# The last output projection: all tiles of y kept on chip for both column halves, and the last tile in two halves

## The chip, the cores and the metric

One core of a Trainium2 chip runs the whole kernel. The metric is the device time of one execution in microseconds (us), as a median of runs. Beside it stands one profiled execution, from which all durations are read.

## What is computed

A two-layer backbone over 1024 latent tokens and 256 context tokens, 1024 wide. Layer 0 runs neighbourhood attention beside mLSTM heads, layer 1 runs 16 heads of a gated linear recurrence (HGRN2). Each layer ends in an output projection, a gate and the residual:

```python
def merge(o, z):                                   # layer 1
    o = _rms(jnp.swapaxes(o, 1, 2).astype(z.dtype), h_norm.reshape(HG_HEADS, HG_VDIM))
    return (o.reshape(o.shape[:2] + (HG_VW,)) * jax.nn.silu(z)) @ w_out     # (1024 x 2048) @ (2048 x 1024)
...
x = x + gate * y_lat
```

The change touches the last of these: `y @ w_out`, times the gate, plus x, for the 1024 latent tokens.

## The kernel before

The heads leave their result y transposed in DRAM (`yd2`: 16 heads, 128 rows of a head, 1024 tokens). The projection sums over 16 heads x 128 rows. It is cut in three ways: tokens in 8 tiles of 128 (`tt`), output columns in two halves of 512 (`b`, 1 before 0), the sum in two halves of 8 heads (`q`). The sums over the first 8 heads (q = 0) are made by `out_some` while the heads still run: for b = 1 they stay on chip in `acc`, for b = 0 they go to DRAM in `self.part`. The **last loop** (L1452 and on) does q = 1: first the 8 tiles of b = 1 with the weights `w2`, then the 8 tiles of b = 0 with `w1`.

float32 products are made exactly enough from two parts: `split` (L72) writes a value's rounded part with ScalarE (L74, `copy`) and the rest with VectorE (L75, subtraction), and each product is three matmuls (high x high, high x low, low x high; L745 to L747). A tile is therefore 8 heads x 3 = 24 matmuls of 128 x 128 by 512 columns into one PSUM bank.

`out_y` (L726) loads a tile of y in two pieces of 256 KB through SP's queue into raw buffers (`wraw`, 3 of them in the pool `yp`), and splits each into halves of `yh` and `yl` (2 buffers each). The weights of w1 arrive in the same three raw buffers of `yp`, two pieces (`later`) after each tile of b = 1. So y is loaded and split once for b = 1 and again for b = 0. `out_tile` (L761) then loads x (`oxh`, 3 buffers), and does three VectorE steps on 512 columns: PSUM plus `part` (L770), times the gate `gbc` (L772), plus x (L773). GpSimd's queue stores the tile (L1461).

Pools lie on two sides of the on-chip memory. `wp` and `yp` (with acc, w2, y's tiles, the raw buffers) are on the right. On the left the heads' pool `hg` is closed before the last loop, and the pools `op1` (`op`: oxh, og, gbc) and `wo1` (w1) open in its space. The heads' pool serves last as the raw buffers of w2.

The program is written in the order of the work. A scheduler places each engine's instructions by that order and by when it thinks that their operands are ready. It puts in all waits. Each engine, and each of the queues on which SP and POOL issue transfers, then runs in that fixed order.

Of the kernel before, what the change touches and what calls it, by code (L numbers as in the profile page):

```python
# [13 lines left out]
ALU = mybir.AluOpType  # L14
# [4 lines left out]
P = 128  # L19
D = 1024  # L20
KD = D // P
LAT = 1024
# [24 lines left out]
class Prog:  # L47
# [688 lines left out]
        return yh, yl  # L736


    def out_sum(self, ps, w, tt, qs, ysrc, yp, bufs, ys=None, rp=None):
        mm = self.nc.tensor.matmul  # L740
        for q in qs:
            yh, yl = ys[q] if ys else self.out_y(tt, q, ysrc, yp, bufs, rp)
            for k in range(8):
                kk = (q - qs[0]) * 8 + k
                mm(ps, lhsT=yh[:, k, :], rhs=w.h(kk), start=(kk == 0), stop=False)  # L745
                mm(ps, lhsT=yh[:, k, :], rhs=w.l(kk), start=False, stop=False)  # L746
                mm(ps, lhsT=yl[:, k, :], rhs=w.h(kk), start=False, stop=(kk == 8 * len(qs) - 1))  # L747

    def out_some(self, w, q, order, ysrc, yp, acc, dst):
        for tt in order:
            ps = self.ps("mm", [P, 512])
            self.out_sum(ps, w, tt, (q,), ysrc, yp, 2)
            o = self.t(yp, [P, 512], F32, "ox", 2) if acc is None else acc[:, tt, :]
            self.nc.scalar.copy(o, ps)
            if acc is None:
                self.nc.gpsimd.dma_start(out=dst[tt * P : (tt + 1) * P, 0:512], in_=o)


    def out_tile(self, w, b, tt, ysrc, xsrc, xt, yp, op, bufs, ys=None, part=None):  # L761
        nc = self.nc
        ps = self.ps("mm", [P, 512])
        self.out_sum(ps, w, tt, (0, 1) if part is None else (1,), ysrc, yp, bufs, ys)
        s = slice(b * 512, (b + 1) * 512)
        nc.sync.dma_start(out=xt, in_=xsrc[:, s])  # L766
        g = self.t(op, [P, 512], F32, "og", self.ogb)
        v = 1 if tt >= LAT // P else 0
        if part is not None:
            nc.vector.tensor_tensor(out=part, in0=ps, in1=part, op=ALU.add)  # L770
            ps = part
        nc.vector.tensor_tensor(out=g, in0=ps, in1=self.gbc[:, v, :], op=ALU.mult)  # L772
        nc.vector.tensor_tensor(out=xt, in0=xt, in1=g, op=ALU.add)  # L773


    def gate_bc(self, l, pool, nv, b):
# [433 lines left out]
    def build(self):  # L1210
        self.six = None
        tc, nc, a = self.tc, self.nc, self.a
        dma = nc.sync.dma_start
        with ExitStack() as es:
# [109 lines left out]
            with tc.tile_pool(name="ml", bufs=2) as pool, self.pp.phase(s=2, acc=2):  # L1324
                wq, self.six = {}, [(self.wp, "w", 4)] * 4
                with self.filler(), tc.issue_after(self.at[8]):
                    self.ml_ahead(*ML_AHEAD[-1])
                self.mask = self.t(pool, [P, 2, P], F32, "mmask", 1)
                dma(out=self.mask, in_=a["mmask"])

                def wo(q, b, ring=None):
                    if not ring:
                        ring, self.six = self.six[:8], self.six[8:] + self.six[:8]
                    src = a["woab"][q * D : (q + 1) * D, b * 512 : b * 512 + 512]
                    return self.wblock(None, "wo", [src], 8, 512, ring=ring)

                for g, at in self.ml_all(pool):
                    with self.filler(), tc.issue_after(at.ins):
                        if g in ML_AHEAD:
                            self.ml_ahead(*ML_AHEAD[g])  # L1340
                        if g == 7:
                            rh.close()
                            wr, self.ogb = es.enter_context(ExitStack()), 1
                            yp = wr.enter_context(tc.tile_pool(name="oy", bufs=1, side="right"))
                            acc = self.t(yp, [P, NT, 512], F32, "oacc", 1)
                            self.six = self.six + [(yp, "wo", 7)] * 7
                        for b in (1, 0):
                            if g == ML_OUT[b][0]:
                                wq[b] = wo(0, b)
                            for tt in [t for t, at_g in zip(ML_ORDER, ML_OUT[b]) if at_g == g]:  # L1350
                                self.out_some(wq[b], 0, [tt], self.yd, yp, acc if b else None, self.x1)
                w2 = wo(1, 1)
                self.gate_bc(0, yp, 2, 1)
                for tt in [8, 9, 3, 4, 2, 5, 1, 6, 0, 7]:
                    xt = self.t(yp, [P, 512], F32, "ox", 2)
                    self.out_tile(w2, 1, tt, self.yd, self.xin(tt), xt, yp, yp, 2, part=acc[:, tt, :])
                    nc.gpsimd.dma_start(out=self.x1[tt * P : (tt + 1) * P, 512:D], in_=xt)
            l0.close()
            l1 = es.enter_context(ExitStack())
# [1 line left out]
            with tc.tile_pool(name="op0", bufs=2) as op, ExitStack() as wl:  # L1361
                wl1 = wl.enter_context(tc.tile_pool(name="wo1", bufs=1))
                w1 = wo(1, 0, [(wl1, "wo", 8)] * 8)
                self.zero = self.t(lk, [P, CTX], F32, "gzero", 1)
                nc.vector.memset(self.zero, 0.0)
                self.lmask = self.t(lk, [P, 6, P], U8, "glm8", 1)
                self.lmask0 = self.t(lk, [P, P], F32, "glm0", 1)
                self.ident8 = self.t(lk, [P, P], U8, "ident8", 1)
                nc.vector.tensor_copy(self.ident8, self.ident)
                lm = self.t(op, [P, D], F32, "nx", 3)[:, 0 : 7 * P].rearrange("p (l f) -> p l f", f=P)  # L1370
                dma(out=lm, in_=a["glm"])
                nc.vector.tensor_copy(self.lmask, lm[:, 1:7, :])
                nc.vector.tensor_copy(self.lmask0, lm[:, 0, :])
                self.gate_bc(0, op, 2, 0)
                wr.close()
                right.close()
                self.six = None
                right = es.enter_context(ExitStack())
                self.wp = right.enter_context(tc.tile_pool(name="w1", bufs=2, side="right"))
                rh = right.enter_context(ExitStack())  # L1380
                self.open_h(rh)
                self.rawp = op
                self.slabs, self.ogb = 4, 3
                early = self.wblock(self.wp, "w", [a["wc"][0:512, 3 * 2048 : 3 * 2048 + 256]], 4, 256, op, ring=self.slabs)
                for tt in [8, 9, 4, 5, 6, 7, 0, 1, 2, 3]:
                    xt = self.t(op, [P, D], F32, "ox", 4)
                    dma(out=xt[:, 512:D], in_=self.x1[tt * P : (tt + 1) * P, 512:D])
                    part = self.t(op, [P, 512], F32, "og", 3)
                    dma(out=part, in_=self.x1[tt * P : (tt + 1) * P, 0:512])
                    self.out_tile(w1, 0, tt, self.yd, self.xin(tt), xt[:, 0:512], op, op, 2, part=part)  # L1390
                    if tt < 8:
                        nc.gpsimd.dma_start(out=self.x1[tt * P : (tt + 1) * P, 0:512], in_=xt[:, 0:512])
                    xn = self.t(op, [P, D], F32, "nx", 3)
                    self.norm(xn, xt, op)
                    self.mod_tr(1, [xn], tt, op, self.h_sink(tt * P, P))

            with l1:
# [48 lines left out]
                w2 = wo(1, 1, ring[4:], raw)  # L1446
            self.ogb = 4
            with tc.tile_pool(name="op1", bufs=2) as op, ExitStack() as wl:
                later = []
                wl1 = wl.enter_context(tc.tile_pool(name="wo1", bufs=1))  # L1450
                w1 = wo(1, 0, [(wl1, "wo", 8)] * 8, [yp, 3, "wraw"], later)
                for b, w in ((1, w2), (0, w1)):  # L1452
                    self.gate_bc(1, op, 1, b)
                    for tt in range(8):
                        xt = self.t(op, [P, 512], F32, "oxh", 3)
                        part = acc[:, tt, :]
                        if not b:
                            part = self.t(op, [P, 512], F32, "og", 4)
                            dma(out=part, in_=self.part[tt * P : (tt + 1) * P, :])
                        self.out_tile(w, b, tt, self.yd2, self.x1[tt * P : (tt + 1) * P], xt, yp, op, 2, part=part)  # L1460
                        nc.gpsimd.dma_start(out=a["out"][tt * P : (tt + 1) * P, b * 512 : (b + 1) * 512], in_=xt)  # L1461
                        for ld in later[:2]:
                            ld()
                        later = later[2:]
# [137 lines left out]
```

## Time and profile before

| | us |
|---|---|
| median of 3 runs | 3510.55 (3509.28 to 3517.46) |
| profiled execution, its own time | 3510.13 |
| its span, first to last instruction | 3508.3 |
| start of the last loop's first tile on TensorE | 3405.2 |
| last matmul starts | 3501.76 |

In the profile PE is TensorE's matmuls, PEld its weight loads, DVE VectorE, ACT ScalarE, POOL GpSimd and SP the engine that only issues transfers; SPq, POOLq and so on are their queues. A row of a timeline gives start, duration, engine, line, operation, written tile and read tiles, count, and in brackets how long the engine sat idle before it and what ended that. A row of windows gives the stretch, its length, the busy time of PE, PEld, DVE, ACT and POOL with counts of instructions, the clock that TensorE was granted (1.00 is full), the busy share of the DMA engines and what they moved in GB/s.

### The profile page before, as it was taken

The page shows a single profiled execution, that of the slowest core. Times are in us where ns is not written, and L with a number is a line of the kernel's source. Part 1 is how long each engine was busy: PE and PEld are TensorE (multiplying, and loading weights), DVE is VectorE, ACT ScalarE, POOL GpSimd, SP SyncE. Part 2 cuts the span into 40 slices and gives each one's busy share as a digit, 9 for nine tenths or more (in the row PEclk, how much of TensorE's full clock was granted, in tenths as well). Part 3 has the DMA queues.
Part 4 walks back from the last instruction along what each step waited for, and adds up shares of the span by engine and source line. Part 5 has one row for each costly group of instructions (what it writes and reads, how often), then busy time and mean ns, then how long its engine had stood idle before and what let it go on. Part 6 is the DMA issues. An engine that isn't in the chain of part 4 may idle for free. (4 is left out here: it accounts for less than half of the span.)

```text
span 3508.3 us, 64938 instructions
## 1 busy us (share of the span) xinstructions
PE 3453.9 (98%) x24438; PEld 3146.4 (90%) x24438; DVE 2374.5 (68%) x6009; ACT 1602.3 (46%) x3700; POOL 526.2 (15%) x844
## 2 busy tenths in 40 slices
PE   8999999999999999999999999999999999999999
PEld 5889999999999999988778999989999999999887
DVE  4668856766666654666767766577777767777855
ACT  5532135555445534555547333344444444444442
POOL 3211121222212211211211111000100000010010
PEclk9999999999999999999999999999999999999999
DMA  7552332332323235364484222211211221121346
GB/s 237 168 160 88 115 90 58 91 87 68 84 77 83 83 88 160 121 183 145 124 258 143 100 103 103 82 37 56 61 48 49 61 61 49 52 64 49 116 146 204
DMA packets 374409, 363.91 MB, mean 104 GB/s; under 512 B 30296, under 2 KB 323096, under 8 KB 373968
## 3 DMA queue, kind: packets, MB, share of 16 engines
q1 hardware_dynamic: 330096, 250.34, 24.4%
q0 software_dynamic: 44000, 109.42, 9.1%
q8 instruction: 193, 3.16, 0.4%
q14 instruction: 120, 0.98, 0.1%
HBM read 276.09 MB, written 83.42 MB: 102 GB/s over the span
## 5 line engine op out<-in xcount | busy, mean ns | idle before, releaser
L127 PE MATMUL mm<-wh,hh 128*128 128x256 f32 x2256 | 649.0, 288 | 4.6 <-DVE ev L922 2.7
L128 PE MATMUL mm<-wl,hh 128*128 128x256 f32 x2256 | 649.0, 288 | 1.9 <-DVE wl L75 1.8
L129 PE MATMUL mm<-wh,hl 128*128 128x256 f32 x2256 | 648.5, 288 | 0.0
L129 PE MATMUL mm<-hh,wl 128*128 128x512 f32 (+1 forms) x1344 | 491.5, 366 | 0.0
L127 PE MATMUL mm<-hh,wh 128*128 128x512 f32 (+1 forms) x1344 | 485.1, 361 | 0.0
L128 PE MATMUL mm<-hl,wh 128*128 128x512 f32 (+1 forms) x1344 | 483.6, 360 | 0.0
L127 PEld LDWEIGHTS mm<-wh,hh 128*128 128x128 f32 x2256 | 431.4, 191 | 12.7 <-issue 6.9
L128 PEld LDWEIGHTS mm<-wl,hh 128*128 128x128 f32 x2256 | 431.6, 191 | 7.2 <-DVE wl L75 2.7
L129 PEld LDWEIGHTS mm<-wh,hl 128*128 128x128 f32 x2256 | 431.1, 191 | 3.6 <-issue 0.7
L74 ACT CAST wh<-wraw 128x512 fp32r<-128x512 f32 x290 | 178.2, 620 | 263.1 <-PE mm L128 130.7
L128 PEld LDWEIGHTS mm<-hl,wh 128*128 128x128 f32 x1344 | 254.0, 189 | 32.0
L129 PEld LDWEIGHTS mm<-hh,wl 128*128 128x128 f32 x1344 | 253.9, 189 | 30.5 <-issue 0.2
L127 PEld LDWEIGHTS mm<-hh,wh 128*128 128x128 f32 x1344 | 254.3, 189 | 29.3
L1109 ACT COPY gksel<-gK 128x512 f32<-128x512 f32 x224 | 147.1, 663 | 218.9 <-PE s L1118 197.6
L75 DVE TENSOR_TENSOR wl<-wraw,wh 128x512 fp32r<-128x512 f32 x290 | 196.5, 686 | 51.9 <-ACT wh L74 49.4
L1118 PE MATMUL s<-gQ,gksel 128*128 128x128 f32 x1536 | 199.9, 276 | 0.0
L1118 PEld LDWEIGHTS s<-gQ,gksel 128*128 128x128 f32 x1536 | 192.4, 191 | 6.9
L745 PE MATMUL mm<-woh,yh 128*128 128x512 f32 x412 | 166.7, 405 | 6.7 <-ACT yh L74 6.5
L747 PE MATMUL mm<-woh,yl 128*128 128x512 f32 x412 | 165.3, 402 | 0.5 <-DVE yl L75 0.5
L746 PE MATMUL mm<-wol,yh 128*128 128x512 f32 x412 | 164.0, 399 | 0.0
L74 ACT CAST wh<-b 128x512 fp32r<-128x512 f32 x124 | 77.0, 622 | 187.1 <-PE sa L129 85.3
L1139 DVE TENSOR_TENSOR gQ<-gQ,gT 128x256 f32<-128x256 f32 x384 | 143.2, 414 | 26.1 <-PE s L1118 26.0
(456 smaller groups left out, 8491.9 us busy)
## 6 DMA issues: line engine op xcount, KB each, us to landing
wraw<-yd SPq DMA_DIRECT2D x144, 256.0 KB
wraw<-in_wc_dram SPq DMA_DIRECT2D x128, 256.0 KB
wraw<-in_wab_dram SPq DMA_DIRECT2D x98, 256.0 KB
md<-ev POOLq DMA_DIRECT2D x94, 256.0 KB, 2.8
adar<-in_wada_dram POOLq DMA_DIRECT2D x32, 512.0 KB, 4.9
b<-in_wc_dram SPq DMA_DIRECT2D x64, 256.0 KB
vzd<-qo POOLq DMA_DIRECT2D x56, 256.0 KB, 2.5
adar<-in_wada_dram SPq DMA_DIRECT2D x16, 512.0 KB
```

Of the source, the lines that this page charges most:

```text
L74: nc.scalar.copy(hi, x)
L75: nc.vector.tensor_tensor(out=lo, in0=x, in1=hi.bitcast(F32), op=ALU.subtract)
L127: mm(ps, lhsT=lh(k), rhs=rh(k), start=(first and k == 0), stop=False)
L128: mm(ps, lhsT=lh(k), rhs=rl(k), start=False, stop=False)
L129: mm(ps, lhsT=ll(k), rhs=rh(k), start=False, stop=(last and k == nk - 1))
L745: mm(ps, lhsT=yh[:, k, :], rhs=w.h(kk), start=(kk == 0), stop=False)
L746: mm(ps, lhsT=yh[:, k, :], rhs=w.l(kk), start=False, stop=False)
L747: mm(ps, lhsT=yl[:, k, :], rhs=w.h(kk), start=False, stop=(kk == 8 * len(qs) - 1))
L1109: nc.scalar.copy(ksel.rearrange("p (b s i) -> p b s i", s=2, i=h), pick(K))
L1118: nc.tensor.matmul(pa[:, c, :].rearrange("p (b s i) -> p b s i", s=2, i=h), lhsT=ksel[:, c * P : (c + 1) * P], rhs=qp[:, c * nbc : (c + 1) ...
L1139: nc.vector.tensor_tensor(out=t[:, i, :, s, :], in0=t[:, i, :, s, :], in1=bc(tot), op=ALU.mult)
```

## The change

`out_sum` becomes `out_part`, which takes a tile of y that has been made already, and a range of columns. Every caller makes y with `out_y` first. In the last loop, y's 8 tiles are made during b = 1 and kept in `ys` for b = 0: tiles 0 and 1 in `yp` (2 buffers), tiles 2 to 7 in `op` (6 buffers), that is, in the space that the heads left. Their raw buffers are then three of `op`'s own; w1's raw pieces stay in `yp`. In `out_tile`, x's load comes ahead of the matmuls. The last tile of b = 0 (`cuts` = 2) is done in two halves of 256 columns: `part` times the gate plus x is formed ahead of its matmuls, each half then takes two VectorE steps (PSUM times gate, plus that), and the halves are stored by SP's and ScalarE's queues.

```diff
-    def out_sum(self, ps, w, tt, qs, ysrc, yp, bufs, ys=None, rp=None):
+    def out_part(self, ps, w, y, ks, cols=slice(0, 512)):
         mm = self.nc.tensor.matmul
-        for q in qs:
-            yh, yl = ys[q] if ys else self.out_y(tt, q, ysrc, yp, bufs, rp)
...
+        yh, yl = y
+        for k in ks:
+            mm(ps, lhsT=yh[:, k, :], rhs=w.h(k)[:, cols], start=(k == 0), stop=False)
+            mm(ps, lhsT=yh[:, k, :], rhs=w.l(k)[:, cols], start=False, stop=False)
+            mm(ps, lhsT=yl[:, k, :], rhs=w.h(k)[:, cols], start=False, stop=(k == 7))
...
-    def out_tile(self, w, b, tt, ysrc, xsrc, xt, yp, op, bufs, ys=None, part=None):
-        nc = self.nc
-        ps = self.ps("mm", [P, 512])
-        self.out_sum(ps, w, tt, (0, 1) if part is None else (1,), ysrc, yp, bufs, ys)
-        s = slice(b * 512, (b + 1) * 512)
-        nc.sync.dma_start(out=xt, in_=xsrc[:, s])
+    def out_tile(self, w, b, tt, y, xsrc, xt, op, part, cuts=0):
+        nc = self.nc
+        tto, gbc = nc.vector.tensor_tensor, self.gbc[:, 1 if tt >= LAT // P else 0, :]
         g = self.t(op, [P, 512], F32, "og", self.ogb)
...
+        nc.sync.dma_start(out=xt, in_=xsrc[:, b * 512 : (b + 1) * 512])
+        if cuts:
+            tto(out=part, in0=part, in1=gbc, op=ALU.mult)
+            tto(out=part, in0=part, in1=xt, op=ALU.add)
+        n = 512 // max(1, cuts)
+        for c in range(0, 512, n):
+            s = slice(c, c + n)
+            ps = self.ps("mm", [P, n])
+            self.out_part(ps, w, y, range(8), s)
+            if not cuts:
+                tto(out=part, in0=ps, in1=part, op=ALU.add)
+                ps = part
+            tto(out=g[:, s], in0=ps, in1=gbc[:, s], op=ALU.mult)
+            tto(out=xt[:, s], in0=xt if not cuts else part[:, s], in1=g[:, s], op=ALU.add)
...
-                later = []
+                later, ys, dma_end = [], {}, (nc.sync, nc.scalar)
...
-                        self.out_tile(w, b, tt, self.yd2, self.x1[tt * P : (tt + 1) * P], xt, yp, op, 2, part=part)
-                        nc.gpsimd.dma_start(out=a["out"][tt * P : (tt + 1) * P, b * 512 : (b + 1) * 512], in_=xt)
+                        if b:
+                            ys[tt] = self.out_y(tt, 1, self.yd2, *((yp, 2) if tt < 2 else (op, 6)))
+                        cuts = 0 if b or tt < 7 else 2
+                        self.out_tile(w, b, tt, ys[tt], self.x1[tt * P : (tt + 1) * P], xt, op, part, cuts)
+                        for c in range(max(1, cuts)):
+                            s, n = slice(tt * P, (tt + 1) * P), 512 // max(1, cuts)
+                            e = nc.gpsimd if not cuts else dma_end[c]
+                            e.dma_start(out=a["out"][s, b * 512 + c * n : b * 512 + c * n + n], in_=xt[:, c * n : c * n + n])
```

The other callers of these functions, `out_some` and the two loops at the end of layer 0 (L1356 and L1390), are rewritten for the new parameters alone.

More of the change, by code (lines that the diff above doesn't have):

```diff
@@ L736, in out_y @@
         return yh, yl
-    def out_sum(self, ps, w, tt, qs, ysrc, yp, bufs, ys=None, rp=None):
+    def out_part(self, ps, w, y, ks, cols=slice(0, 512)):
         mm = self.nc.tensor.matmul
-        for q in qs:
-            yh, yl = ys[q] if ys else self.out_y(tt, q, ysrc, yp, bufs, rp)
[L743 to L747, printed above, removed]
+        yh, yl = y
[3 more added lines that the diff above has]
+            mm(ps, lhsT=yl[:, k, :], rhs=w.h(k)[:, cols], start=False, stop=(k == 7))
     def out_some(self, w, q, order, ysrc, yp, acc, dst):
@@ L753, in out_some @@
             ps = self.ps("mm", [P, 512])
-            self.out_sum(ps, w, tt, (q,), ysrc, yp, 2)
+            y = self.out_y(tt, q, ysrc, yp, 2)
+            self.out_part(ps, w, y, range(8))
             o = self.t(yp, [P, 512], F32, "ox", 2) if acc is None else acc[:, tt, :]
@@ L758, in out_some @@
                 self.nc.gpsimd.dma_start(out=dst[tt * P : (tt + 1) * P, 0:512], in_=o)
-    def out_tile(self, w, b, tt, ysrc, xsrc, xt, yp, op, bufs, ys=None, part=None):
+    def out_tile(self, w, b, tt, y, xsrc, xt, op, part, cuts=0):
         nc = self.nc
-        ps = self.ps("mm", [P, 512])
-        self.out_sum(ps, w, tt, (0, 1) if part is None else (1,), ysrc, yp, bufs, ys)
-        s = slice(b * 512, (b + 1) * 512)
-        nc.sync.dma_start(out=xt, in_=xsrc[:, s])
+        tto, gbc = nc.vector.tensor_tensor, self.gbc[:, 1 if tt >= LAT // P else 0, :]
         g = self.t(op, [P, 512], F32, "og", self.ogb)
[L768 to L773, printed above, removed]
+        nc.sync.dma_start(out=xt, in_=xsrc[:, b * 512 : (b + 1) * 512])
[12 more added lines that the diff above has]
+            tto(out=xt[:, s], in0=xt if not cuts else part[:, s], in1=g[:, s], op=ALU.add)
     def gate_bc(self, l, pool, nv, b):
@@ L1355, in build @@
                     xt = self.t(yp, [P, 512], F32, "ox", 2)
-                    self.out_tile(w2, 1, tt, self.yd, self.xin(tt), xt, yp, yp, 2, part=acc[:, tt, :])
+                    self.out_tile(w2, 1, tt, self.out_y(tt, 1, self.yd, yp, 2), self.xin(tt), xt, yp, acc[:, tt, :])
                     nc.gpsimd.dma_start(out=self.x1[tt * P : (tt + 1) * P, 512:D], in_=xt)
@@ L1389, in build @@
                     dma(out=part, in_=self.x1[tt * P : (tt + 1) * P, 0:512])
-                    self.out_tile(w1, 0, tt, self.yd, self.xin(tt), xt[:, 0:512], op, op, 2, part=part)
+                    self.out_tile(w1, 0, tt, self.out_y(tt, 1, self.yd, op, 2), self.xin(tt), xt[:, 0:512], op, part)
                     if tt < 8:
```

## The prediction, on record before the result

> **What bounds the kernel now.** I read the page first, then the windows of the last stretch, then TensorE's timeline there for gaps, then the DMA queue (SPq) and the engines around those gaps, and last the chain behind the final matmul. The page's first lines:
>
> ```profile
> span 3508.3 us, 64938 instructions
> PE 3453.9 (98%) x24438; PEld 3146.4 (90%) x24438; DVE 2374.5 (68%) x6009; ACT 1602.3 (46%) x3700; POOL 526.2 (15%) x844
> ```
>
> TensorE bounds the whole: 98% busy. So the change can gain only where PE waits, runs slowly, or has ended. The changed loop begins at 3405.2 us; its windows (first 8 tiles up to a regained pace, the rest of them, the second 8, the tail; columns as "us, PE, PEld, DVE, ACT, POOL busy, clock, DMA share, GB/s"):
>
> ```profile
> 3405.20:3440.70 35.50, 30.21 (x122) 23.02 (x120) 20.24 (x31) 12.07 (x20) 2.70 (x5) 0.95 0.67 204
> 3440.70:3457.02 16.32, 16.32 (x74) 13.52 (x72) 9.38 (x15) 3.66 (x7) 1.62 (x3) 1.00 0.70 208
> 3457.02:3502.16 45.14, 45.13 (x193) 35.97 (x191) 24.10 (x38) 8.67 (x14) 4.32 (x8) 1.00 0.66 209
> 3502.16:3508.40 6.24, 0.00 (x0) 0.00 (x0) 2.08 (x3) 0.00 (x0) 0.54 (x1) 0.70 0.22 84
> ```
>
> PE lacks 5.3 us in the first window and nothing in the next two. In the second 8 tiles y is loaded and split again, but behind a full PE: dropping that work (16 loads, 16 casts, 16 subtractions) is worth nothing by itself. The gaps, on PE's timeline, with tile starts (24 matmuls each):
>
> ```profile
> 3410.65 0.39 PE L745 MATMUL mm<-woh,yh 128*128 128x512 f32 x1
> 3419.48 0.79 PE L745 MATMUL mm<-woh,yh 128*128 128x512 f32 x1 [3.23 <-ACT yh L74]
> 3422.72 0.39 PE L746 MATMUL mm<-wol,yh 128*128 128x512 f32 x1
> 3428.13 0.50 PE L745 MATMUL mm<-woh,yh 128*128 128x512 f32 x1 [1.36 <-ACT yh L74]
> 3434.85 0.50 PE L745 MATMUL mm<-woh,yh 128*128 128x512 f32 x1 [0.69 <-ACT yh L74]
> 3440.70 0.39 PE L745 MATMUL mm<-woh,yh 128*128 128x512 f32 x1
> 3446.14 0.39 PE L745 MATMUL mm<-woh,yh 128*128 128x512 f32 x1
> ```
>
> A tile without a wait takes 3446.14 - 3440.70 = 5.44 us. Tiles 1 to 4 (3410.65 to 3440.70) took 30.05 instead of 4 x 5.44 = 21.76: **8.29 us lost**, more than the gaps. The rest is clock: after the 3.23 us gap the seven steps from 3419.48 to 3422.72 took 3.24 us instead of 7 x 0.227 = 1.59, while this window's granted clock (third number from the end) was 0.55:
>
> ```profile
> 3420.00:3423.00 3.00, 3.00 (x9) 2.05 (x8) 2.52 (x5) 0.62 (x1) 0.44 (x1) 0.55 0.86 236
> ```
>
> The Trainium skill (TensorE: Matmul & The Clock Gate, Part 1: The HAM clock gate) says that an idle window of some 3.4 us halves the clock until about as long has been busy; the trace agrees, 0.55 after 3.23 us idle, for 3.2 us.
>
> Why tile 2 came late:
>
> ```profile
> 3407.23 0.69 DVE L75 TENSOR_TENSOR wol<-wraw,woh 128x512 fp32r<-128x512 f32 x1 [0.32 <-ACT woh L74]
> 3408.06 0.33 SPq L780 DMA_DIRECT2D gbc<-gated  x1
> 3408.44 1.49 SPq L766 DMA_DIRECT2D oxh<-x  x3
> 3410.03 0.90 SPq L103 DMA_DIRECT2D wraw<-in_woc_dram  x2
> 3411.77 7.20 SPq L732 DMA_DIRECT2D wraw<-yd  x2
> 3417.23 1.38 ACT L74 CAST woh<-wraw 128x512 fp32r<-128x512 f32 x2 [6.21 <-DMA wraw<-in_woc_dram]
> 3418.81 0.62 ACT L74 CAST yh<-wraw 128x512 fp32r<-128x512 f32 x1 [0.20 <-DMA wraw<-yd]
> ```
>
> The heads' space opens with the last split from it (3407.92); gbc, three x tiles and two weight pieces go out, and only then tile 2's y, whose second half waits 7 us for one of three raw slots that two weight pieces hold.
>
> **The change, part by part.** *y of tiles 2 to 7 into the heads' space, with a raw ring of its own.* It can start no earlier than 3408, since op opens then. But it waits neither for weights' slots nor for y's two buffers. I expect SP to send gbc, x of tiles 0 and 1, then y of tile 2. In the rows above seven transfers (gbc to the first y) were used 10.75 us after the first was issued, 1.5 us each. As fourth and fifth, tile 2's halves land about 3414.2 and 3415.7 and are split by 3417.0; PE needs them at 3416.09 (3410.65 + 5.44) and, 12 matmuls on, 3418.8. So the long wait goes, and the clock's fall with it. Later tiles have a lead. DMA is near its limit though: up to tile 5's start at 3432.4 there are 24 transfers to move (gbc, 5 x, 8 y, 6 weights, 4 stores), 6.3 MB in 24.3 us or 259 GB/s, against 204 on average in the first window. I leave 1.5 us of short waits, the size of the two shorter gaps (1.36 and 0.69). **Gain 8.3 - 1.5 = 6.8**; bounds 0 and 8.3. x now goes out ahead of its tile's matmuls: on SP the order y, x stays. SP waits for x's slot (oxh, 3 deep) as before; behind that wait stand y loads of later tiles, which have more than a tile's lead.
>
> *Pace of the second 8 tiles.* They run slower per tile than the first: 3496.37 - 3490.75 = 5.62. In layer 0's loop with y and weights both in the left-hand pools, as tiles 2 to 7 will now be, 24 matmuls took 1823.50 - 1818.06 = 5.44:
>
> ```profile
> 3490.75 0.40 PE L745 MATMUL mm<-woh,yh 128*128 128x512 f32 x1
> 3496.37 0.40 PE L745 MATMUL mm<-woh,yh 128*128 128x512 f32 x1
> 1818.06 0.39 PE L745 MATMUL mm<-woh,yh 128*128 128x512 f32 x1
> 1823.50 0.39 PE L745 MATMUL mm<-woh,yh 128*128 128x512 f32 x1
> ```
>
> If placement is the reason, tiles 2 to 6 gain 5 x 0.18 = **0.9**. I take that, as the nearest row; other end: the mixture of pools moves to tiles 2 to 7 of the first half and costs 6 x 0.18 = 1.1.
>
> *The last tile in two halves.* Its 24 matmuls of 512 columns become 48 of 256. Eight such steps of the projections take 0.96 us (first two rows below), so 48 x 0.12 = 5.76 instead of 5.62: **-0.14**. Behind the last matmul stand now three VectorE steps, a POOL store and the closing drain:
>
> ```profile
> 2022.05 0.28 PE L127 MATMUL tr<-wh,hh 128*128 128x256 f32 x1
> 2023.01 0.28 PE L129 MATMUL tr<-wh,hl 128*128 128x256 f32 x1
> 3502.19 0.69 DVE L770 TENSOR_TENSOR og<-mm,og 128x512 f32<-128x512 f32 x1 [1.10 <-PE mm L747]
> 3502.92 0.69 DVE L772 TENSOR_TENSOR og<-og,gbc 128x512 f32<-128x512 f32 x1
> 3503.64 0.69 DVE L773 TENSOR_TENSOR oxh<-oxh,og 128x512 f32<-128x512 f32 x1
> 3504.63 0.54 POOL L1461 DMA_DIRECT2D out_dram<-oxh  x1 [2.70 <-DVE oxh L773]
> L1598 POOLq DRAIN x3: 46/98/2939, 3504.6 to 3508.1; - x3
> L1139 DVE TENSOR_TENSOR gK<-gK,gT 128x256 f32<-128x256 f32 x384 | 143.3, 417 | 1.0 <-ACT gksel L1109 1.0
> ```
>
> The three steps end at 3504.33, 2.14 after they begin; two of 256 columns at 0.417 with a gap of 0.03 take 0.87: **+1.25**. The two steps put ahead (part x gate, + x) are 1.4 us on a VectorE that is half idle (24.1 of 45.1) and have the first half's 2.9 us as cover; without it they would cost their 1.4. The store: from 3504.33 to the drain's end at 3504.6 + 2.94 = 3507.5 it takes 3.2 us for 256 KB. No row has one from ACT's queue. The nearest HWDGE rows are loads through SP: a small one on a quiet chip, issue to use, 2.45 - 0.73 = 1.7 us, and one of 256 KB under load, 3410.40 - 3406.94 = 3.5:
>
> ```profile
> 0.73 0.38 SPq L1239 DMA_DIRECT2D cT<-in_cT_dram  x1
> 2.45 0.22 ACT L1256 ACTIVATE sct<-cT 128x16 f32<-128x16 f32 x1 [0.44 <-DMA cT<-in_cT_dram]
> 3406.94 0.38 SPq L732 DMA_DIRECT2D wraw<-yd  x1
> 3410.40 0.62 ACT L74 CAST yh<-wraw 128x512 fp32r<-128x512 f32 x1 [1.26 <-DMA wraw<-yd]
> ```
>
> I take 2.3, nearer the quiet one, since little else moves (DMA share 0.22 in the tail): **+0.9**, bounds -0.3 and 1.5. By the Trainium skill (DMA: Bandwidth & Descriptors, Specifications) the first byte comes after about 0.6 us on the scalar path and 1 us on GpSimd's, which alone would make this term an estimated 0.4; no run here shows it. The tail's sum is 1.25 + 0.9 - 0.14 = 2.0 (0.8 to 2.6). Nothing is queued behind either store on SP or ACT.
>
> *Layer 0's calls* only get y ahead of the PSUM tile; each engine's own order is the same: nothing, and no cover needed.
>
> Sum: 6.8 + 0.9 + 2.0 = 9.7. The profiled execution took 3510.13 us (span plus 1.83 around it), 0.42 less than the median of the runs, so 3500.4 there and **3500.8** as a median. What a measurement of this kernel can tell from no change is about 0.3%, 10.5 us here: the line lies at 3500.0, just beside the forecast.
>
> **The rivals.** *A, the stall stays.* For it: the space still opens at 3407.92, two weight pieces get their slots at 3410.03 and stand ahead of tile 2 by the program's order, and DMA is near its limit. With tile 2's halves sixth and seventh we are where the trace is now, and only pace and tail come: 3510.55 - 2.9 = 3507.7; half the stall gives 3504. Against it: three x loads got out before those pieces, so there was room ahead of them.
>
> *B, slower: a wait at every tile.* With no buffer to hold it back, y runs ahead and floods the queue, and splits of later tiles stand on VectorE ahead of earlier tiles' additions, which free PSUM (two banks for mm). Each of tiles 2 to 6 then waits for a transfer meant for the next. If such a wait reaches the 3.23 us that slowed the clock above, each costs 3.23 + 1.65 = 4.9, five 24.4, against 8.3 now: 16.1 worse, less 2.9, so 3523.8. It decides from there: waits of 1.4 us without the clock's fall (7 us) only match today. The clock gate's rule in the Trainium skill (same section), by which each idle window is paid again in slow matmuls, is what makes this steep; the trace shows it once, at 0.55. Against it: only three raw slots, so y can run at most one and a half tiles ahead of its splits.
>
> *C, the halves bring nothing:* if the store from ACT takes the loaded 3.5 us and the pace stays, 3510.55 - 6.8 - 0.8 = 3503. That lies within the forecast's case.
>
> **How the numbers follow.** Forecast (with C) 0.64, A 0.25, B 0.11. The forecast's own span is 3498 (no wait left, 8.3 + 0.9 + 2.6 = 11.8, near 3498.7, with some run-to-run spread) to 3504; a little over half of it, 0.35, lies below 3500.0 since the waits left may well be under 0.7 us. Faster 0.35; same 0.29 + 0.25 = 0.54; slower 0.11. The range 3497.5 to 3510 takes in A and leaves out B and a twentieth below.
>
> **What would show it.** Right: no PE gap over 1 us between 3405 and 3450, no window with a clock under 0.9, y loads of tile 2 on SP before the weight pieces, tiles of 5.44 in both halves, two 256-wide VectorE rows and some 4 us between the last matmul and the end (6.1 now). Wrong: a gap of 3 us at tile 2 (A), gaps at each tile (B), 5.6 in the first half (pace), or a last store of over 3 us (C). A shift before 3400 would mean that the order elsewhere changed, which I count at nothing.

## The result and the profile after

The changed kernel takes 3501.7 us (median of 9 runs, 3499.94 to 3503.54); the kernel before, beside it, 3512.32 (9 runs, 3508.71 to 3517.46). The ratio is 0.9969, with a 95% interval from 0.9961 to 0.9978: 10.6 us less, between 7.7 and 13.7. The profiled execution took 3502.94 us, 7.2 less than the one of before. First the page's span and engines:

```profile
span 3501.2 us, 64888 instructions
PE 3451.5 (99%) x24462; PEld 3146.8 (90%) x24462; DVE 2367.3 (68%) x5996; ACT 1592.9 (45%) x3684; POOL 526.2 (15%) x843
```

PE has 24 matmuls more (the last tile's 48 for 24), and its share went from 98% to 99%. Of the 7.1 us that went, 4.7 are idle time (54.4 to 49.7 us) and 2.4 are busy time, which is where matmuls at a fallen clock are counted. The windows of the last loop, in four stretches like those shown of before (first half up to tile 6, the end of the first half, second half, tail), and under them a narrow one around the start of tile 2; columns as before, the clock third from the end:

```profile
3404.50:3441.56 37.06, 35.31 (x146) 28.05 (x145) 24.21 (x38) 14.56 (x24) 2.72 (x6) 0.95 0.74 230
3441.56:3452.75 11.19, 11.19 (x49) 9.01 (x48) 4.16 (x6) 0.00 (x0) 1.60 (x3) 1.00 0.33 119
3452.75:3497.12 44.37, 44.37 (x217) 37.26 (x215) 18.66 (x28) 0.00 (x0) 4.32 (x8) 1.00 0.43 146
3497.12:3501.20 4.08, 0.00 (x0) 0.00 (x0) 0.85 (x2) 0.00 (x0) 0.00 (x0) 0.97 0.10 32
3420.00:3423.00 3.00, 3.00 (x10) 2.35 (x9) 3.00 (x6) 1.86 (x3) 0.54 (x1) 0.59 0.78 253
```

PE lacks 1.75 us in the first stretch where it lacked 5.3, and nothing in the next two. ScalarE has nothing left to do in the second half, DMA is busy 0.43 of it instead of 0.66, and the tail is 4.08 us instead of 6.24. But the clock still fell once, to 0.59. PE's timeline, starts of tiles 1, 2, 3, 4 and 5 of the first half, 2, 3 and 7 of the second, and the last matmul:

```profile
3409.94 0.39 PE L743 MATMUL mm<-woh,yh 128*128 128x512 f32 x1
3417.29 0.47 PE L743 MATMUL mm<-woh,yh 128*128 128x512 f32 x1 [1.75 <-issue]
3424.76 0.39 PE L743 MATMUL mm<-woh,yh 128*128 128x512 f32 x1
3430.36 0.39 PE L743 MATMUL mm<-woh,yh 128*128 128x512 f32 x1
3435.96 0.39 PE L743 MATMUL mm<-woh,yh 128*128 128x512 f32 x1
3469.44 0.39 PE L743 MATMUL mm<-woh,yh 128*128 128x512 f32 x1
3474.88 0.39 PE L743 MATMUL mm<-woh,yh 128*128 128x512 f32 x1
3491.20 0.28 PE L743 MATMUL mm<-woh,yh 128*128 128x256 f32 x1
3496.84 0.28 PE L745 MATMUL mm<-woh,yl 128*128 128x256 f32 x1
```

One gap of 1.75 us stands where there were three (3.23, 1.36, 0.69). Tile 1 takes 7.35 us up to tile 2's start, tile 2 7.47 although no gap follows: part of its matmuls ran at the fallen clock. Tiles 3 and 4 take 5.60, not 5.44; tile 2 of the second half takes 5.44, not 5.62: for these tiles the two halves of the columns have changed places. What tile 2 waited for, in SP's queue (with issue times) and on ScalarE:

```profile
3407.54 0.33 SPq L783 DMA_DIRECT2D gbc<-gated  x1
3407.91 1.02 SPq L763 DMA_DIRECT2D oxh<-x  x2
3408.98 0.43 SPq L732 DMA_DIRECT2D wraw<-yd  x1
3409.52 1.65 SPq L103 DMA_DIRECT2D wraw<-in_woc_dram  x2
3416.57 0.62 ACT L74 CAST yh<-wraw 128x512 fp32r<-128x512 f32 x1 [5.84 <-DMA wraw<-yd]
```

Its first piece is the fourth transfer and goes out at 3408.98, 4.5 us behind the loop's start. Before, it went out at 3411.77, 6.6 us behind the loop's start, when a raw buffer came free. With the change it is used 7.6 us after its issue, and ScalarE idles 5.84 us for it. The tail: VectorE's two steps, the store from ScalarE's queue, and the closing drains of SP, whose first start is taken here as the sign that the last store has landed:

```profile
3497.15 0.42 DVE L775 TENSOR_TENSOR og<-mm,gbc 128x256 f32<-128x256 f32 x1 [1.39 <-PE mm L745]
3497.61 0.43 DVE L776 TENSOR_TENSOR oxh<-og,og 128x256 f32<-128x256 f32 x1
3498.07 0.38 ACTq L1470 DMA_DIRECT2D out_dram<-oxh  x1
L1607 SPq DRAIN  x3: 7/7/13, 3500.3 to 3500.6; - x3
```

VectorE ends at 3498.04, 0.89 us after it began (2.14 before); the store takes 2.26 us from there (3.2 before).

The whole loop, cut at tile starts, in us; the column "again" is a second profile of the same changed kernel (e11 below), cut at 3408.88, 3414.32, 3437.70, 3492.92 and 3502.9:

| stretch | before | after | again |
|---|---|---|---|
| tile 0 | 5.44 | 5.44 | 5.44 |
| tiles 1 to 4 of the first half | 30.05 | 26.02 | 23.38 |
| from there to the last tile's start | 55.67 | 55.24 | 55.22 |
| last tile to the end of the span | 11.93 | 10.00 | 9.98 |
| loop | 103.1 | 96.7 | 94.0 |

The loop gained 6.4 us in one profile and 9.1 in the other. The loop's start, up to which all compared kernels but one run their matmuls in the same order, lay between 3401.8 and 3410.1 us over this study's profiles. So a total carries several us that the change has no part in, and the loop is the sharper measure of it.

### The profile page after: what moved, and what is told of

Same layout as the page of the kernel before. It is cut to its first block, busy times and chain, and to the rows that moved or that the text cites. A ratio compares the mean times of both kernels' runs of the same rounds, so it can differ in the third digit from the quotient of the medians.

```text
span 3501.2 us, 64888 instructions
## 1 busy us (share of the span) xinstructions
PE 3451.5 (99%) x24462; PEld 3146.8 (90%) x24462; DVE 2367.3 (68%) x5996; ACT 1592.9 (45%) x3684; POOL 526.2 (15%) x843
## 4 chain that ended last, share of the span: by engine, by line
PE 88%; issue 5%; DMA 2%; ACT 2%; DVE 1%; POOL 1%; SPq 0%; POOLq 0%; ACTq 0%; DVEq 0%
PE mm L129 15%; PE mm L128 15%; PE mm L127 15%; PE s L1121 6%; PE mm L743 3%; PE mm L744 3%; PE mm L745 3%; PE acc L695 3%; PE tr L675 2%; PE sa L128 2%; PE sa L127 2%; PE sa L129 2%; PE acc L478 2%; PE s L485 2%; PE s L1166 1%
## 5 line engine op out<-in xcount | busy, mean ns | idle before, releaser
L743 PE MATMUL mm<-woh,yh 128*128 128x512 f32 (+1 forms) x420 | 167.7, 400 | 2.7 <-issue 1.7
L745 PE MATMUL mm<-woh,yl 128*128 128x512 f32 (+1 forms) x420 | 166.4, 397 | 0.4 <-DVE yl L75 0.3
L744 PE MATMUL mm<-wol,yh 128*128 128x512 f32 (+1 forms) x420 | 165.7, 395 | 0.0
```

Source lines behind the costliest of these rows:

```text
L743: mm(ps, lhsT=yh[:, k, :], rhs=w.h(k)[:, cols], start=(k == 0), stop=False)
L744: mm(ps, lhsT=yh[:, k, :], rhs=w.l(k)[:, cols], start=False, stop=False)
L745: mm(ps, lhsT=yl[:, k, :], rhs=w.h(k)[:, cols], start=False, stop=(k == 7))
```

## The experiments

The theory is the prediction's: raw buffers of its own let tile 2's y out ahead of the weights; the sides on which operands lie set the pace; two halves shorten the tail. Against it stand these: that merely fewer transfers matter, that the broadcast of the gate is what delays tile 2, and that the tail's gain comes from the store's queue alone. Each kernel is the changed one with the edit shown. Ratios are to the kernel before, with 95% intervals. "Loop" is the time from the first matmul of the last loop to the end of the span, 103.1 before, 96.7 and 94.0 with the change. Totals of single executions are not compared.

**e1: keep y, no halves.**

```diff
-                        cuts = 0 if b or tt < 7 else 2
+                        cuts = 0
```

> y kept on chip as in the change, but the last tile whole and stored by GpSimd. My theory (the gain of the kept y is the shorter wait at tiles 2 to 4, the tail's gain is its own): the stretch before the last matmul as in the changed kernel (about 3.9 us lost at tiles 1 and 2, one gap of 1.5 to 2 us), 5.44 for the last tile, and 6.1 us from the last matmul to the end instead of 4.1; so about 2 us above the changed kernel, 3503 to 3505. Rival (nearly all of the gain is the tail): within 2 us of the kernel before, 3509 or more.

Measured: 3504.16 us, ratio 0.9975 (0.9966 to 0.9985); loop 96.0. Tile 2's gap and the last matmul:

```profile
3418.38 0.47 PE L743 MATMUL mm<-woh,yh 128*128 128x512 f32 x1 [0.64 <-issue]
3496.17 0.39 PE L745 MATMUL mm<-woh,yl 128*128 128x512 f32 x1
```

The gap is 0.64 us here, under the 1.5 to 2 expected, and tiles 1 and 2 took 6.24 and 6.13. From the last matmul's start to the end of the span (3502.7) it is 6.53, as before (6.54), against 4.36 with the halves. Keeping y carries the first half's gain, and the halves carry the tail's.

**e2: halves, y not kept.** y is loaded again in the second half.

```diff
-                        if b:
-                            ys[tt] = self.out_y(tt, 1, self.yd2, *((yp, 2) if tt < 2 else (op, 6)))
+                        ys[tt] = self.out_y(tt, 1, self.yd2, yp, 2)
```

> Only the last tile in halves; y loaded again for the second column half with two buffers as before. My theory: gaps of some 3, 1.4 and 0.7 us at tiles 2 to 4 and about 8 us lost there, all tiles of the second half at 5.62, 4.1 us behind the last matmul: 2 us below the kernel before, some 3510. Rival (all from the tail): as fast as the changed kernel, 3501 to 3503.

Measured: 3510.5 us, ratio 0.9991 (0.9982 to 1.0); loop 102.9, no better than before. PE's first wait, then the last tile's two halves, SP's last loads, and the addition that the second half waited for:

```profile
3415.61 0.50 PE L743 MATMUL mm<-woh,yh 128*128 128x512 f32 x1 [2.77 <-ACT yh L74]
3492.42 0.28 PE L743 MATMUL mm<-woh,yh 128*128 128x256 f32 x1
3497.39 0.39 PE L743 MATMUL mm<-woh,yh 128*128 128x256 f32 x1 [2.00 <-DVE og L773]
3492.55 0.32 SPq L763 DMA_DIRECT2D oxh<-x  x1
3492.92 0.90 SPq L1462 DMA_DIRECT2D og<-part  x2
3496.65 0.69 DVE L773 TENSOR_TENSOR og<-mm,og 128x512 f32<-128x512 f32 x1 [2.31 <-DMA og<-part]
```

The stall is back (tiles 1 to 4 lost 7.7 us), as expected. The tail is short (4.47 from the last matmul's start), but the last tile's matmuls took 7.81 us from the first start to the last, against 5.64 with the change. Two PSUM banks serve `mm`. The second half needs the one that tile 6 holds until L773 has added `part`, and `part` was asked for only at 3492.92. It stood in SP's queue behind the load of x at 3492.55, for which SP had waited 4.0 us until an earlier tile's store gave its x buffer free. In the changed kernel, with y neither loaded nor split in the second half, both `part` loads are out by 3487.7 and PE has no such gap. Whether y's loads on SP or its splits on VectorE made this chain late was not tried. So "dropping that work is worth nothing by itself" was wrong in this combination: without it the halves give their 2 us back.

**e3: y kept, but its raw buffers shared with the weights.**

```diff
-                            ys[tt] = self.out_y(tt, 1, self.yd2, *((yp, 2) if tt < 2 else (op, 6)))
+                            ys[tt] = self.out_y(tt, 1, self.yd2, *((yp, 2) if tt < 2 else (op, 6)), rp=yp)
```

> The change, but the raw pieces of y for tiles 2 to 7 go through the same three raw buffers as the weights of w1, as before. My theory (the shared raw slots held tile 2 up): the gap at tile 2 is 3 us or more again, 7 to 9 us lost at tiles 1 to 4, some 4 us above the changed kernel, 3505 to 3507. Rival (y's two buffers held it up, not the raw slots): as the changed kernel, one gap under 2 us.

Measured: 3509.62 us, above the 3505 to 3507 expected; ratio 0.9992 (0.9983 to 1.0002), loop 100.6. Starts of tiles 1, 2, 3 and 4, and tile 2's two loads on SP:

```profile
3413.97 0.39 PE L743 MATMUL mm<-woh,yh 128*128 128x512 f32 x1
3421.98 0.47 PE L743 MATMUL mm<-woh,yh 128*128 128x512 f32 x1 [2.41 <-issue]
3431.02 0.51 PE L743 MATMUL mm<-woh,yh 128*128 128x512 f32 x1 [2.65 <-ACT yh L74]
3438.35 0.39 PE L743 MATMUL mm<-woh,yh 128*128 128x512 f32 x1
3415.52 5.98 SPq L732 DMA_DIRECT2D wraw<-yd  x2
```

Three tiles took 24.4 us, 8 more than 3 x 5.44, with two long gaps. With everything else of the change in place the stall is whole again, and tile 2's loads stand on SP as before: behind three x loads and two weight pieces, with 5.98 us until both are out. The shared raw buffers caused it, and the separate ones removed most of it; the number of transfers did not.

**e4: the gate's broadcast for the first half ahead of the first-eight-heads loops.**

```diff
+                self.gate_bc(1, yp, 1, 1)
                 for i, b in enumerate((1, 0)):
...
-                    self.gate_bc(1, op, 1, b)
+                    if not b:
+                        self.gate_bc(1, op, 1, b)
```

> The change, with the gate row of the first column half loaded earlier, into the right-hand pool, while the heads' work still runs; so two x tiles are left ahead of tile 2's first y load in the burst that starts when the heads' space opens. Theory 1 (the gate's broadcast of one row to 128 partitions is slow and holds up what is queued behind it): tile 2's first y piece is used 5 us or less after its issue instead of 7.6, no gap at tile 2, no fall of the clock, about 4 us below the changed kernel (3497 to 3499). Theory 2 (bytes alone: one of four transfers less): 6 to 6.5 us from issue to use, a gap of 0.3 to 0.9 us left, 1 to 3 us below the changed kernel.

Measured: 3504.78 us, ratio 0.9976 (0.9964 to 0.9987); loop 93.3. Tile 2's start:

```profile
3423.10 0.47 PE L743 MATMUL mm<-woh,yh 128*128 128x512 f32 x1 [0.21 <-ACT woh L74]
```

The gap shrank to 0.21, and tiles 1 and 2 took 5.81 and 5.69. But this edit also changed the order of the heads' matmuls. The stretch between the first and the last of the heads' copies by ScalarE (L1098) grew from 1039.8 us, with the change, to 1042.0, and the loop began later, at 3411.85. The loop did what was expected, the total did not. Nor does one profile show the loop's part to be the edit's: in e11 and e8, which leave this order alone, the gap at tile 2 was 0.46 and none.

**e5: tile 2's y made ahead of the gate's broadcast.** One execution.

```diff
                 for b, w in ((1, w2), (0, w1)):
+                    if b:
+                        ys[2] = self.out_y(2, 1, self.yd2, op, 6)
...
-                        if b:
+                        if b and tt != 2:
```

> The change, with tile 2's y asked for ahead of the gate row and the x tiles; each engine's matmul order stays. Theory 1 (tile 2 is late because of what is queued ahead of it): its first piece is used 4 us or less after its issue, no gap at tile 2, tiles 1 and 2 together lose under 1 us instead of 3.9; the gate row comes later, so that VectorE's first step with the gate waits longer, without a gap on the matmul engine. Theory 2 (what is in flight shares the rate, order matters little): 6 us or more from issue to use, and a gap of 1 us or more stays.

Measured: 3500.88 us; loop 93.5. Both of tile 2's loads on SP, its first split, and the starts of tiles 1 and 3:

```profile
3408.36 1.09 SPq L732 DMA_DIRECT2D wraw<-yd  x2
3412.38 0.62 ACT L74 CAST yh<-wraw 128x512 fp32r<-128x512 f32 x1 [1.09 <-DMA wraw<-yd]
3411.03 0.39 PE L743 MATMUL mm<-woh,yh 128*128 128x512 f32 x1
3422.43 0.39 PE L743 MATMUL mm<-woh,yh 128*128 128x512 f32 x1
```

Sent first, the piece was used 4.0 us after its issue, and tiles 1 and 2 together took 11.40 us (2 x 5.44 is 10.88). e12, which has the same edit, shows 4.0 us too. So the place of tile 2's y in SP's queue counts in what is left of the stall with the change.

**e6 and e7: the sides.** In e6 the kept y goes to a pool on the right, where w2 lies; in e7 w1 does too (its pool line below with `side="right"`), so that everything lies on one side. Order and instructions are those of the change.

```diff
+                yr = wl.enter_context(tc.tile_pool(name="yr", bufs=1, side="right"))
...
-                            ys[tt] = self.out_y(tt, 1, self.yd2, *((yp, 2) if tt < 2 else (op, 6)))
+                            ys[tt] = self.out_y(tt, 1, self.yd2, *((yp, 2) if tt < 2 else (yr, 6)), rp=yp if tt < 2 else op)
```

```diff
-                wl1 = wl.enter_context(tc.tile_pool(name="wo1", bufs=1))
+                wl1 = wl.enter_context(tc.tile_pool(name="wo1", bufs=1, side="right"))
```

> The change, with the six kept tiles of y in a pool on the right, the weights of the second half on the left as before; the order on every engine is the same. Theory 1 (a matmul is slower when its two operands lie on different sides): tiles without a wait take 5.44 us in the first half and 5.62 in the second, tiles 2 to 6 too. Theory 2 (y in the heads' space is what is slow): 5.60 in the first half from tile 3 on, as in the changed kernel.

> The change, with the six kept tiles of y and the weights of the second half both in pools on the right; the order on every engine is the same. Theory 1 (different sides are slow): 5.44 us for every whole tile without a wait, some 1.4 us gained on the changed kernel over the loop, too little for the runs' spread to show surely: 3500 to 3502. Theory 2 (the addresses of the heads' space are slow against the old ones): 5.60 in the first half from tile 3 on, 5.62 for tiles 0 and 1 of the second, no gain.

Measured: e6 3504.08 us (one execution), loop 95.8; e7 3500.3 us, ratio 0.9969 (0.9958 to 0.998), loop 93.0. Rows 24 matmuls apart, two of the first half and two of the second, first e6, then e7:

```profile
3425.38 0.39 PE L743 MATMUL mm<-woh,yh 128*128 128x512 f32 x1
3430.82 0.39 PE L743 MATMUL mm<-woh,yh 128*128 128x512 f32 x1
3469.99 0.39 PE L743 MATMUL mm<-woh,yh 128*128 128x512 f32 x1
3475.61 0.40 PE L743 MATMUL mm<-woh,yh 128*128 128x512 f32 x1
```

```profile
3422.83 0.39 PE L743 MATMUL mm<-woh,yh 128*128 128x512 f32 x1
3428.27 0.39 PE L743 MATMUL mm<-woh,yh 128*128 128x512 f32 x1
3450.24 0.39 PE L743 MATMUL mm<-woh,yh 128*128 128x512 f32 x1
3455.68 0.39 PE L743 MATMUL mm<-woh,yh 128*128 128x512 f32 x1
```

e6: 5.44 where y and w2 are both right, 5.62 where y is right and w1 left. e7: 5.44 in both halves. With the change it was 5.60 (y left, w2 right), then 5.44 (both left). Four combinations, one rule: operands on different sides cost 3%. In its total e7 can't be told apart from the change: 6 x 0.16 + 2 x 0.18 = 1.3 us is less than the intervals are wide. In both, tiles 5 and 6 of the first half still lost 0.1 to 0.4 us each to short waits.

e6 shows something else besides. SP's order around tile 2 is that of the change, and so is the gap, but the clock did not fall:

```profile
3419.25 0.47 PE L743 MATMUL mm<-woh,yh 128*128 128x512 f32 x1 [1.72 <-issue]
3422.00:3425.00 3.00, 3.00 (x14) 2.15 (x13) 3.00 (x6) 1.86 (x3) 0.54 (x1) 1.00 0.73 236
```

Tile 2 took 6.13 us here, 0.69 over a full pace; with the change it took 7.47, 1.87 over its full pace of 5.60.

**e8: the last tile's two stores from GpSimd.** One execution.

```diff
-                            e = nc.gpsimd if not cuts else dma_end[c]
+                            e = nc.gpsimd
```

> The change, with both halves of the last tile stored by GpSimd's queue instead of SP's and ScalarE's. Theory 1 (the queue counts): the closing stretch from the last matmul's start to the end is 0.9 us longer than the changed kernel's 4.36, 5.0 to 5.5. Theory 2 (only the smaller store and the shorter VectorE steps count): 4.3 to 4.8.

Measured: 3504.46 us; loop 94.1. Last matmul and last store:

```profile
3497.78 0.28 PE L745 MATMUL mm<-woh,yl 128*128 128x256 f32 x1
3499.27 0.54 POOL L1470 DMA_DIRECT2D out_dram<-oxh  x1 [1.73 <-DVE oxh L776]
```

From the last matmul's start to the end of the span (3502.7) it is 4.92 us, about 0.6 longer than with ScalarE's store and just under the 5.0 to 5.5 that the first theory gave. Some 0.3 of that is a later issue: GpSimd's begins 0.30 us after VectorE has ended (3498.97), ScalarE's 0.03. So of some 0.9 that the store gained, about 0.6 is the queue's; that the rest goes with its halved size is a conclusion by difference.

**e9: the gate's broadcast early, but behind the first-eight-heads loops.**

```diff
                 w2 = wo(1, 1, ring[4:], raw)
+                self.gate_bc(1, yp, 1, 1)
...
-                    self.gate_bc(1, op, 1, b)
+                    if not b:
+                        self.gate_bc(1, op, 1, b)
```

> The change, with the gate row of the first half in the right-hand pool and asked for behind w2's weights, so that the matmul engine's order is untouched (in the run with the gate loaded earlier it was not). Theory: as in that run, tile 1 and 2 lose under 1 us instead of 3.9 and the clock stays, while the time ahead of the loop is that of the changed kernel: some 3 us below it, 3497.5 to 3500. Rival (an early gate row always costs 3 us ahead of the loop): 3503 to 3506 again.

Measured: 3502.37 us, ratio 0.9973 (0.9962 to 0.9984); loop 94.0. Tile 2's start:

```profile
3419.02 0.47 PE L743 MATMUL mm<-woh,yh 128*128 128x512 f32 x1 [0.86 <-ACT woh L74]
```

The heads' matmuls kept their order, and of e4's delay ahead of the loop only 0.4 us came. But the gap is 0.86, inside what the change itself shows from run to run. No total gain is seen. In e4 and e9 tile 2's first piece was used 5.1 and 5.6 us after its issue, against 6.0 to 7.7 in runs with the broadcast ahead of it; that it is slow in itself, more than any transfer one place ahead, is not shown.

**e11: the changed kernel once more.** One execution, no edit.

> The changed kernel once more, to see how much of the wait at tile 2 and of the clock's fall differs from run to run. Theory: the gap is set by where the transfers stand and is 0.6 to 1.9 us again, as in the runs that share its order; the clock falls only when the gap meets the gate's window, so tiles 1 and 2 lose between 1.3 and 3.9 us together. Rival: 1.9 and 3.9 again within 0.3.

Measured: 3504.65 us; loop 94.0. Tile 2's start, and a window behind it:

```profile
3420.37 0.47 PE L743 MATMUL mm<-woh,yh 128*128 128x512 f32 x1 [0.46 <-issue]
3421.00:3424.00 3.00, 3.00 (x13) 2.17 (x12) 3.00 (x6) 1.87 (x3) 0.00 (x0) 1.00 1.05 304
```

The same program had a gap of 0.46 instead of 1.75, a little under the 0.6 expected, and its clock was 1.00 in that window. Its total is higher than the first profile's all the same: the loop began 4.4 us later.

**e12: e5 and e7 together.** Beside the two pool lines of e7:

```diff
+                    if b:
+                        ys[2] = self.out_y(2, 1, self.yd2, yr, 6, rp=op)
...
-                        if b:
+                        if b and tt != 2:
```

> The change with both of what helped: tile 2's y asked for first, and y's kept tiles and the second half's weights in pools on the right. Theory (the two are separate: one takes the wait of tiles 1 and 2, the other the slow pace): under 1 us lost in tiles 1 and 2, 5.44 us for every whole tile, some 91.5 to 92.5 us from tile 0's start to the end of the span instead of 96.7: 4 to 5 us below the changed kernel, 3496 to 3499. Rival (the runs' spread ahead of the loop hides it): within 2 us of the changed kernel.

Measured: 3502.05 us, ratio 0.9971 (0.996 to 0.9982); loop 92.7, the shortest of all. The loop's first matmul and the first of tile 2:

```profile
3410.09 0.39 PE L743 MATMUL mm<-woh,yh 128*128 128x512 f32 x1
3421.42 0.47 PE L743 MATMUL mm<-woh,yh 128*128 128x512 f32 x1 [0.29 <-DMA oxh<-x]
```

Tiles 0 and 1 took 11.33 us, with a gap of 0.29, and tiles 1 and 2 lost 0.5 us. Tiles 3, 5 and 6 of the first half still lost 0.1 to 0.3 each; all whole tiles of the second half took 5.44. In the loop it is 1.3 us ahead of the change's better profile, but in its total it can't be told apart from the change. No version was shown to beat it.

## Why the prediction was right, and where not

The forecast of 3500.8 lies 0.9 us from the median, and the measured ratio of 0.9969 lies close to the 0.3% at which the text had drawn its line; its interval leaves out 1. But the forecast took 9.7 us off a median of 3510.55, and 10.6 were measured off one of 3512.32. The steps are less exact than that sum:

| term, us | forecast | after | again (e11) |
|---|---|---|---|
| stall | 6.8 | 4.5 | 7.2 |
| pace | 0.9 | -0.1 | -0.1 |
| tail | 2.0 | 1.93 | 1.95 |
| loop | 9.7 | 6.4 | 9.1 |

*Stall.* The mechanism is shown by e3: with shared raw buffers, the stall; with separate ones, most of it gone. In the account of before one thing was left out. Tile 2 waited for its first piece (split at 3418.81), not for the second with its 7 us in the queue. That first piece, too, stood until a raw buffer came free: the one that VectorE's split of tile 1's second piece released at 3411.74. SP's order was as forecast for tile 2's first half (fourth). Its second half went seventh, behind two weight pieces, instead of fifth. That cost little: in e11 it shows as two steps of some 0.33 us instead of 0.23, half-way through tile 2. The failing step is the rate of 1.5 us per transfer, which put the first half at 3414.2: it was used at 3416.57, 7.6 us after its issue, and 6.0 to 6.7 after it in e11, e8, e1 and e7, 7.7 in e6. While it was under way (3408.98 to 3416.57) DMA moved 286 GB/s, 2.2 MB or some eight such pieces, so the fourth in the queue did not land after four shares of the rate; how the transfers share it is not shown. Nor was DMA near its limit at the 259 GB/s of the text: between 3413 and 3416 it moved 367. What is left of the stall in tiles 1 and 2, beside a full pace, was 3.8 us in after, 2.6 in e6, 1.3 in e1, 1.2 in e7, 1.1 in e11 and 0.6 in e8, which all have the same order on SP: 1.8 on average, against 1.5 forecast. So the term was right in the mean and rough in each run, and "no gap over 1 us", which was to show it, held in four of these six. "No window with a clock under 0.9" failed in after.

*Pace.* This term failed. The forecast had the two ends, +0.9 for the second half and -1.1 for the first, as alternatives and took one; they come together. Tiles 2 to 7 of the first half now have y left and weights right and lose 6 x 0.16; tiles 2 to 6 of the second have both left and win 5 x 0.18. The sum is -0.06. That placement is the reason, which the text took as an "if", is what e6 and e7 show.

*Tail.* All its parts came out near their prices: 48 steps of 0.12 (3491.20 to 3496.84 and one more), 1.25 on VectorE, 0.94 for the store with 2.26 against 2.3 assumed. The Trainium skill (DMA: Bandwidth & Descriptors, Specifications) would have given an estimated 0.4 for the store from the difference of the first bytes alone; e8 measures about 0.6 for the change of queue. What the text did not see is the condition that e2 shows: with y loaded and split again the second half waits 2.0 us for PSUM.

*The rivals.* A, the stall stays, is what e3 does, at 3509.62, near the 3507.7 given for A; the change avoids it. B, a wait at each tile, did not come: no gap follows tile 2 in either profile of the change. C, no gain from the halves, fails by e1 against the change, 6.53 to 4.36 in the tail.

*What stays open.* The medians differ by 10.6 us, the loops by 6.4 to 9.1. Part of this is where the profiled executions lie: the one of before (3510.13) is 2.2 us under its median, the one of after (3502.94) 1.2 over its own. e2, whose loop gained 0.2, also has a median 3.2 us lower (0 to 6.3). From the first of the heads' copies (L1098) to the loop's start it is 1092.7 to 1092.8 us in before, in after and in every other profile except e4 (1095.2) and e9 (1093.2). So the spread of the loop's start arises earlier than that. Whether the kernel before loses something there that its one profile does not show, or the spread accounts for all of it, was not settled. So the nearness of the total to the forecast is partly luck: the loop's mean gain, 7.7, is 2 us under the forecast.

## What to carry to other kernels

Raw buffers shared by two streams let the one that was issued first hold up the one that is due first; look in the DMA queue for loads that are long in going out (tile 2's two took 7.20 us before and 5.98 in e3; with the change they took 0.43 and 0.56), and give each stream its own. Work that seems to cost nothing can, once it is dropped, be what lets another edit pay (e2), so price the two together. Where the spread ahead of a stretch exceeds what an edit is worth, compare that stretch from its first matmul, in more than one profile.

## What the runs showed of the hardware that was not expected

Matmuls of 512 columns whose operands lie on different sides start 0.233 to 0.234 us apart (5.60 and 5.62 / 24), and 0.227 where both lie on one side, left or right (5.44 / 24); why is not known, and whether the side or the distance of the addresses decides was not tried.

The clock fell to 0.59 after a gap of only 1.75 us in after, but stayed at 1.00 behind gaps of 1.72 in e6 and 2.41 in e3. It fell to 0.50 behind gaps of 2.65 (e3), 2.77 (e2) and 3.23 (before). So between 1.7 and 2.4 us the length of the gap alone does not decide. Nor does the fall come with the gap: in after PE resumed at 3417.29, its steps were back at 0.23 us by 3418.31, and only then went to 0.43, from 3419.38 to 3422.37. The Trainium skill (TensorE: Matmul & The Clock Gate, Part 1: The HAM clock gate) gives some 3.4 us of idle window as the condition, with a window that runs freely; every gap here was shorter than that, and what decided in each case is not shown. A gap's price is thus not proportional to its length: 1.75 us of gap left 3.8 us lost with the clock's fall, 1.72 left 2.6 without it, 0.46 left 1.1.

The same load of 256 KB took 4.0 us from issue to use when it went first in its burst and 6.0 to 7.7 when it went fourth.
